# An encoder's MLP: its up projections with tokens on partitions, turned by VectorE and moved by GpSimd's DMA queue

## The chip, the cores and the metric

The kernel runs on one NeuronCore of a Trainium2 chip. The metric is the device time of one execution in microseconds (us); lower is better. A core has TensorE (PE, matrix products into PSUM), VectorE (DVE), ScalarE (ACT), GpSimd (POOL) and SyncE (SP); the last two also issue DMAs here, each on a queue of its own.

## The reference

Two layers on 256 tokens of 1024 channels, in float32. Each layer has a token mixer (pooling windows, dilated attention, gates) and then a gated MLP with a convolution of three tokens:

```python
def _conv_ffn(xn, w_up, conv_w, conv_b, w_down):
    a, gval = jnp.split(xn @ w_up, 2, axis=-1)          # D_FF = 2816 each
    a = depthwise_conv(a, conv_w, width 3, centred) + conv_b
    return (jax.nn.gelu(a) * gval) @ w_down

h = h + _token_mixer(_rmsnorm(h, norm1[layer]), ...)
h = h + _conv_ffn(_rmsnorm(h, norm2[layer]), ...)
```

The convolution runs over tokens, channel by channel.

## The kernel before

Channels are cut into blocks of 128: 8 for the model's width, 22 (NF) for D_FF. Every weight is read from HBM once, in loads of 1 MB. Each load is used as two pieces of 1024 values per partition. A piece is split into a high part (a rounding to the matrix engine's float32r, made by ScalarE, L179) and a low part (the rest, made by VectorE, L180). Activations are split in the same way, and a product is the sum of high x high, high x low and low x high. The class Weights keeps the order: `use` lists the pieces in the order of their use, `get` returns the next one and splits up to three ahead (LOOK = 3, five buffers BUFS, three load buffers RAW). A piece may go to a slot of an idle tile instead of one of the five buffers. A framework orders the instructions of each engine and sets the semaphores; tiles with one tag share a place in memory, so a new tile waits for the readers of the old one.

There are two forms of projection. `proj` (L489) has channels on the partitions of its result: the weight block stands in the array and the 256 tokens, high and low together 512 columns, stream through (L485); the weight's low part sees the high tokens alone, 256 columns (L487). `by_rows` (L587, through `v_sum` L577 and L582) has tokens on the partitions: a block of activations stands in the array and 512 columns of weights stream through, six matmuls for a piece and half of the tokens (t = 0, 1), four pieces for 512 columns. Its result must be turned before the convolution, which needs tokens in the free direction.

The MLP before the change takes the last four blocks of a (ENTRY = 4, the rest are FIRST = 18) by rows, at its start, in two PSUM tiles; ScalarE copies them, and VectorE turns them in 16 small transposes of 32 partitions (`blocks` L607, L612), one after each projection. All the other blocks, 18 of a and 22 of g, come from `proj`, two loads with 256 columns for two blocks. `up(f)` (L1124) adds the two sums of a block (ScalarE copies one, L507, VectorE adds the other, L508), convolves (L1134, L1135, L1138), applies the gelu by its tanh form (L1147 to L1152), multiplies by g (L1155), and splits the result (L1160, L1161). The down projection `residual_mm` (L516) takes one block per step: 12 matmuls of 512 columns (L512 to L514) into four PSUM tiles. It starts after block 6 (LAG) and goes on by two steps for every two blocks. The last four steps (`hold`) are held back, and are then run part by part, so that the norm of the first tokens can start early.

The mixer turns attention weights and its merged branch by VectorE's 32 x 32 transposes followed by `cross` (L599): 16 DMAs within SBUF that move each group of 32 partitions to its place, four after each visit, on SP's queue (L604). SP's queue also carries every load of weights (L119).

Of the kernel before, what the change touches and what calls it, by code (L numbers as in the profile page):

```python
# [10 lines left out]
F32 = mybir.dt.float32  # L11
# [24 lines left out]

WARM = (5, 1, 2, 1)
PAIRS = (2, 4, 0, 1, 3, 5)
LAG = 6
VISITS = ((0, 1, 12, 14), (2, 3, 15, 16), (9, 10, 22, 23), (10, 11, 23, 24))  # L40
ENTRY = 4
FIRST = NF - ENTRY
HALVES = (slice(0, 512), slice(512, D))
SEGMENTS = (HALVES, (slice(0, 512), slice(512, 768), slice(768, D)))

# [37 lines left out]
class Weights:  # L83
# [27 lines left out]
    def load(self, upto):  # L111
        while self.n_loaded < min(upto, len(self.loads)):
            src, shape, tag = self.loads[self.n_loaded]
            name = f"raw{self.n_loaded}"
            if tag is None:
                t = self.pool.tile([P, *shape], F32, tag="raw", bufs=self.RAW, name=name)
            else:
                t = self.idle.tile([P, *shape], F32, tag=tag, name=name)
            self.nc.sync.dma_start(out=t, in_=src)  # L119
            self.raw[self.n_loaded] = t  # L120
            self.n_loaded += 1

# [84 lines left out]
def encoder(ctx, tc, x, w_in, w_pool, pool_scale, w_a, w_b, w_o, norm1, norm2, w_up, conv_w,  # L207
# [28 lines left out]

    for l in range(DEPTH):
        for g in range(NG):
            c0 = C_V + g * 512
            slots = (("m2", 0, 2), ("m2", 1, 2), ("ybig",), ("at2",)) if g == 0 else ()  # L240
            for j in range(2):
                tag = "k1" if l == 0 and g == 1 and j == 0 else None
                W.use(rows(w_in[l], j * 512, 4, c0, 512, tag), slots[2 * j : 2 * j + 2])
        if l == 0:
            W.n_scaled = len(W.pieces)
        for c in range(3, -1, -1):
            W.use(cols(w_in[l], c * 256))
        for n, c in enumerate(PAIRS):
            q = cols(w_in[l], C_Q + c * 256)
            if n == 1:  # L250
                pool = W.add(
                    w_pool[l].rearrange("g (k p) c -> p (g k) c", p=P), (8, 256),
                    [((lambda t, j=j: t[:, 4 * j : 4 * j + 4, :]), (4, 256)) for j in range(2)],
                )
            k = cols(w_in[l], C_K + c * 256)
            if n == 1:
                k.insert(1, pool[0])
            if n == 2:
                q.insert(1, pool[1])
            W.use(q + k)  # L260
        def half_of(w, c0, half, n):
            for j in range(n):
                W.use(rows(w, j * 512, 4, c0 + half.start, 512))

        for half in HALVES:
            half_of(w_in[l], C_GP, half, 2)
        for half in HALVES:
            half_of(w_a[l], 0, half, 2)
            half_of(w_in[l], C_GA, half, 2)
            half_of(w_b[l], 0, half, 1)  # L270
        for c in range(4):
            W.use(rows(w_o[l], c * 256))
        slots = (("v1",), ("ybig",), ("at2",))
        for j in range(2):
            W.use(rows(w_up[l], j * 512, 4, FIRST * P, 512), slots[2 * j : 2 * j + 2])
        for f in range(0, NF, 2):
            a = cols(w_up[l], f * P) if f < FIRST else []
            g = cols(w_up[l], DFF + f * P)
            W.use([a[0], g[0], a[1], g[1]] if a else g)
            if f >= LAG:  # L280
                W.use(rows(w_down[l], (f - LAG) * P))
        for f in range(NF - LAG, NF, 2):
            W.use(rows(w_down[l], f * P))


    h = const.tile([P, 2, D], F32, name="h")
# [214 lines left out]
    def in_order(a):  # L501

        return a.rearrange("p (m t) -> p t m", t=2)

    def add_up(out, sums):

        nc.scalar.copy(out=out, in_=sums[1])  # L507
        nc.vector.tensor_add(out=out, in0=sums[0], in1=out)  # L508
# [65 lines left out]
    def v_tile():  # L574
        return acc.tile([P, 512], F32, tag="acc", name="v_ps")

    def v_sum(ps, x2, t, n, piece, of=4):  # L577

        _, (wh, wl) = piece
        passes = [(0, wh, 0), (0, wl, 0), (1, wh, 0), (0, wh, 1), (0, wl, 1), (1, wh, 1)]  # L580
        for m, (part, w, j) in enumerate(passes):
            nc.tensor.matmul(  # L582
                ps, x2[:, 2 * n + j, part, t, :], w[:, j, :], start=(n + m == 0),
                stop=(n == of - 1 and m == 5),
            )
# [13 lines left out]
    def cross(out, in_):  # L599

        for i in range(4):
            for j in range(4):
                a, b = slice(32 * i, 32 * i + 32), slice(32 * j, 32 * j + 32)
                nc.sync.dma_start(out=out[b, i], in_=in_[a, j])  # L604
            yield

    def blocks(out, in_):  # L607

        for i in range(4):
            for j in range(4):  # L610
                a, b = slice(32 * i, 32 * i + 32), slice(32 * j, 32 * j + 32)
                nc.vector.transpose(out=out[b, :, :, a], in_=in_[a, :, :, b])  # L612
                yield
# [166 lines left out]
    for l in range(DEPTH):  # L780
# [326 lines left out]
        acts = {}  # L1107


        a_last = big.tile([P, ENTRY, S], F32, tag="gates", name="a_last")  # L1110
        a_rows = big.tile([P, 2, ENTRY, P], F32, tag="m2", name="a_rows")

        held, ps = entry
        for t in range(2):
            if t:
                ps = v_tile()
                for n in range(4):
                    v_sum(ps, x2, t, n, held[n])
            nc.scalar.copy(out=a_rows[:, t], in_=ps)
        for i, _ in held:  # L1120
            W.free(i)
        turning = blocks(a_last.rearrange("p f (m t) -> p t f m", t=2), a_rows)

        def up(f):  # L1124
            w0, w1, w2, b = (prm[:, l, j * NF + f : j * NF + f + 1] for j in range(4))
            if f >= FIRST:
                a = a_last[:, f - FIRST, :]
            else:
                a = sm.tile([P, S], F32, tag="u", name="a")
                add_up(in_order(a), [halves(b) for b in proj(x2)])  # L1130
                next(turning, None)
            sums = proj(x2)
            y = sm.tile([P, S], F32, tag="s", name="y")
            nc.scalar.activation(y, a, AF.Identity, bias=b, scale=w1)  # L1134
# [3 lines left out]
            nc.vector.scalar_tensor_tensor(  # L1138
                out=y[:, : S - 1], in0=a[:, 1:], scalar=w2, in1=y[:, : S - 1],
                op0=ALU.mult, op1=ALU.add,  # L1140
            )
# [37 lines left out]
        for f in range(0, NF, 2):  # L1179
            up(f)  # L1180
            up(f + 1)
            if f >= LAG:
# [38 lines left out]
```

## Time and profile before

| | |
|---|---|
| median of 3 runs | 870.25 us (870.25 to 870.68) |
| the profiled execution | 870.25 us, of which its span is 868.5 us |
| granted TensorE clock | 0.998 |
| TensorE busy | 860.7 us |
| VectorE busy | 670.5 us |
| ScalarE busy | 496.8 us |
| GpSimd busy | 21.1 us |
| DMA | 167.23 MB, mean 193 GB/s |

The span runs from the first to the last instruction of the profiled execution. A group of the profile reads: line, engine, operation, result <- sources (partitions x elements) x count | busy us, mean ns of one | idle time of the engine just before, and what ended it. A row of a timeline reads: start, length, engine, line, operation. A matmul's end is modelled and overlaps the next one's start, so lengths add up to more than the time that passes. The chain of waits is followed back from the last instruction. A row of DMA issues ends with the size of one transfer and the median time from issue to landing.

### The profile page before, as it was taken

How to read it: one execution, taken by the hardware profiler on the slowest of the kernel's cores; microseconds unless marked ns; L12 is line 12 of the kernel's file. 1: busy time of each engine (PE TensorE's matmuls, PEld its weight loads, DVE VectorE, ACT ScalarE, POOL GpSimd, SP SyncE). 2: the span in 40 equal slices, each digit the busy share in tenths (PEclk: the TensorE clock that was granted, in tenths of full speed). 3: DMA queues.
4: the chain of work that ended last, by engine and by line, in shares of the span. 5: the costliest groups of instructions: out<-in, count | busy, mean ns of one | idle time of the engine just before them, and what ended most of it. 6: DMA issues, size and time to landing. Idle time of an engine off the chain costs nothing.

```text
span 868.5 us, 12204 instructions
## 1 busy us (share of the span) xinstructions
PE 860.7 (99%) x4554; PEld 740.9 (85%) x4554; DVE 670.5 (77%) x1084; ACT 496.8 (57%) x817; POOL 21.1 (2%) x53
## 2 busy tenths in 40 slices
PE   9999999999999999999999999999999999999997
PEld 7888988888888888888888899888888888888885
DVE  6998795756759997789756968775557799887884
ACT  6755644544646775667545555454445467666662
POOL 2020000000010000000000000000000000000000
PEclk9999999999999999999999999999999999999999
DMA  9676636664745565555626455547558255664631
GB/s 326 210 210 229 223 118 223 189 222 158 270 155 194 185 203 193 197 193 194 242 98 225 163 195 194 173 167 241 186 203 274 96 183 200 223 205 155 198 141 49
DMA packets 116095, 167.23 MB, mean 193 GB/s; under 512 B 4846, under 2 KB 81854, under 8 KB 116036
## 3 DMA queue, kind: packets, MB, share of 16 engines
q1 hardware_dynamic: 115524, 165.12, 56.6%
q0 software_dynamic: 496, 1.33, 0.6%
q8 instruction: 36, 0.59, 0.3%
q14 instruction: 23, 0.19, 0.1%
q10 hardware_dynamic: 16, 0.00, 0.0%
HBM read 160.12 MB, written 1.07 MB: 186 GB/s over the span
## 4 chain that ended last, share of the span: by engine, by line
PE 99%; ACT 0%; POOLq 0%; DVE 0%; issue 0%; POOL 0%; ACTq 0%
PE proj_ps L485 30%; PE rows_ps L582 18%; PE proj_ps L487 16%; PE res_ps L512 6%; PE res_ps L513 6%; PE v_ps L582 6%; PE res_ps L514 6%; PE v_ps L772 3%; PE v_ps L685 1%; PE o_ps L963 1%; PE s_ps L906 1%; PE o_ps L959 1%; PE s_ps L901 1%; PE xt_ps L453 1%; PE pool_ps L479 0%; PE pool_ps L478 0%
## 5 line engine op out<-in xcount | busy, mean ns | idle before, releaser
L180 DVE TENSOR_TENSOR wl<-raw,wh 128x1024 fp32r<-128x1024 f32 x274 | 333.1, 1222 | 121.0 <-ACT wh L179 118.4
L179 ACT CAST wh<-raw 128x1024 fp32r<-128x1024 f32 x274 | 285.6, 1049 | 173.0 <-PE proj_ps L485 64.7
L485 PE MATMUL proj_ps<-x,wh 128*128 128x512 f32 x1152 | 288.4, 392 | 0.0
L485 PEld LDWEIGHTS proj_ps<-x,wh 128*128 128x128 f32 x1152 | 208.2, 189 | 38.0
L487 PEld LDWEIGHTS proj_ps<-x,wl 128*128 128x128 f32 x1152 | 157.2, 190 | 11.3
L487 PE MATMUL proj_ps<-x,wl 128*128 128x256 f32 x1152 | 160.8, 282 | 0.0
L582 PE MATMUL rows_ps<-wh,x 128*128 128x512 f32 x256 | 82.1, 393 | 0.0
L512 PE MATMUL res_ps<-wh,actq 128*128 128x512 f32 (+1 forms) x184 | 70.2, 381 | 0.0
L513 PE MATMUL res_ps<-wl,actq 128*128 128x512 f32 (+1 forms) x184 | 70.1, 381 | 0.0
L514 PE MATMUL res_ps<-wh,actk 128*128 128x512 f32 (+1 forms) x184 | 69.9, 380 | 0.0
L582 PEld LDWEIGHTS rows_ps<-wh,x 128*128 128x128 f32 x256 | 47.9, 188 | 9.7
L582 PE MATMUL rows_ps<-wl,x 128*128 128x512 f32 x128 | 49.9, 389 | 0.0
L514 PEld LDWEIGHTS res_ps<-wh,actk 128*128 128x128 f32 x184 | 34.6, 188 | 6.7
L582 PE MATMUL rows_ps<-wh,po 128*128 128x512 f32 x128 | 40.1, 389 | 0.0
L512 PEld LDWEIGHTS res_ps<-wh,actq 128*128 128x128 f32 x184 | 34.7, 188 | 6.2
L513 PEld LDWEIGHTS res_ps<-wl,actq 128*128 128x128 f32 x184 | 34.7, 188 | 6.0
L1134 ACT ACTIVATE y<-a,prm 128x256 f32<-128x256 f32 x36 | 21.6, 600 | 21.9 <-DVE a L508 21.9
L1151 ACT ACTIVATE y<-y 128x256 f32<-128x256 f32 x44 | 18.3, 416 | 21.4 <-DVE y L1148 21.2
L582 PEld LDWEIGHTS rows_ps<-wh,po 128*128 128x128 f32 x128 | 24.0, 188 | 5.0
L582 PEld LDWEIGHTS rows_ps<-wl,x 128*128 128x128 f32 x128 | 24.1, 188 | 4.8
L512 PE MATMUL res_ps<-wh,m 128*128 128x512 f32 (+1 forms) x72 | 26.9, 374 | 0.0
L419 ACT ACTIVATE junk<-h 128x512 f32<-128x512 f32 (+1 forms) x20 | 10.9, 547 | 27.1 <-DVE h L417 27.1
(209 smaller groups left out, 1155.0 us busy)
## 6 DMA issues: line engine op xcount, KB each, us to landing
raw<-in_w_in_dram SPq DMA_DIRECT2D x58, 1024.0 KB, 5.2
raw<-in_w_up_dram SPq DMA_DIRECT2D x44, 1024.0 KB, 4.9
raw<-in_w_down_dram SPq DMA_DIRECT2D x22, 1024.0 KB, 4.9
raw<-in_w_a_dram SPq DMA_DIRECT2D x8, 1024.0 KB, 5.8
raw<-in_w_o_dram SPq DMA_DIRECT2D x8, 1024.0 KB, 7.1
pt<-rows SPq DMA_DIRECT2D x64, 64.0 KB, 3.7
raw<-in_w_b_dram SPq DMA_DIRECT2D x4, 1024.0 KB
raw<-in_w_pool_dram SPq DMA_DIRECT2D x2, 1024.0 KB
```

The source lines that it names most:

```text
L179: lambda: nc.scalar.copy(out=h, in_=src),
L180: lambda: nc.vector.tensor_sub(out=l, in0=src, in1=h.bitcast(F32)),
L419: nc.scalar.activation(junk[:, 0 : cc.stop - cc.start], h[:, t, cc], AF.Square, scale=D**-0.5, accum_out=ss[:, n : n + 1],)
L485: nc.tensor.matmul(ps, wh(k), x2[:, k], start=(k == 0), stop=False)
L487: nc.tensor.matmul(ps[:, 1], wl(k), x2[:, k, 0], start=False, stop=(k == nk - 1))
L512: nc.tensor.matmul(ps, ah, wh, start=first, stop=False)
L513: nc.tensor.matmul(ps, ah, wl, start=False, stop=False)
L514: nc.tensor.matmul(ps, al, wh, start=False, stop=last)
L582: nc.tensor.matmul(ps, x2[:, 2 * n + j, part, t, :], w[:, j, :], start=(n + m == 0), stop=(n == of - 1 and m == 5),)
L772: nc.tensor.matmul(ps[t], a[:, k, t, :], w[:, j, :], start=(k + m == 0), stop=(k == KD - 1 and m == 2),)
L1134: nc.scalar.activation(y, a, AF.Identity, bias=b, scale=w1)
L1151: nc.scalar.activation(y2, y2, AF.Tanh, scale=c)
```

## The change

All of the up projection goes by rows, in eleven sets of 512 columns per layer: a0 to a4 and g0 to g4 with four blocks each, and r5 with the last two blocks of a and of g (its two loads of 1 MB are cut in two halves each). ORDER gives the order of sets and of groups of four down steps (d0 to d4). A unit is one weight piece. CHUNKS gives for each block the unit after which `up` is called. At a set's end VectorE turns both PSUM tiles (one for each half of the tokens) in 32 x 32 blocks into one of two buffers (`up_at2`), and `cross` moves the blocks: for a and r into a tile in the place of `gates` or `v0`, for g into one of two buffers in the place of `xn`. `up` then starts with a scalar copy that brings a into token order (in place of the two sums), and multiplies by g straight from the turned tile; the factor 0.5 of the gelu moves from that product into the split. `cross` issues on GpSimd's queue in place of SP's, in the mixer too.

```diff
-LAG = 6
+ORDER = "a0 g0 a1 g1 a2 g2 d0 a3 g3 d1 a4 g4 r5 d2 d3 d4"
+CHUNKS = (13, 15, 17, 19, 21, 23, 25, 27, 29, 31, 33, 35, 41, 43, 45, 47, 53, 54, 56, 57, 58, 60)
-ENTRY = 4
-FIRST = NF - ENTRY
...
     def cross(out, in_):
         for i in range(4):
             for j in range(4):
                 a, b = slice(32 * i, 32 * i + 32), slice(32 * j, 32 * j + 32)
-                nc.sync.dma_start(out=out[b, i], in_=in_[a, j])
+                nc.gpsimd.dma_start(out=out[b, i], in_=in_[a, j])
             yield
...
+        def turn_up(key, ps, tag):
+            if not ways:
+                for own in ("at2", "xn"):
+                    t = big.tile([P, 2, 4, 2, 4, 32], F32, tag=own, name="up_" + own)
+                    ways.append([t[:, 0], t[:, 1]])
+            rows = ways[0].pop(0)
+            ways[0].append(rows)
+            if tag is None:
+                out = ways[1].pop(0)
+                ways[1].append(out)
+            else:
+                out = big.tile([P, 4, 2, 4, 32], F32, tag=tag, name="up_turned")
+            for t in range(2):
+                nc.vector.transpose(
+                    out=rows[:, :, t].rearrange("p j c r -> p c j r"),
+                    in_=ps[t].rearrange("p (c j r) -> p c j r", c=4, j=4),
+                )
+            run(cross(out, rows))
+            turned[key] = out.rearrange("p i t c r -> p c t i r")
...
         def up(f):
-            if f >= FIRST:
-                a = a_last[:, f - FIRST, :]
-            else:
-                a = sm.tile([P, S], F32, tag="u", name="a")
-                add_up(in_order(a), [halves(b) for b in proj(x2)])
-                next(turning, None)
-            sums = proj(x2)
+            n, c = divmod(f, 4)
+            av, gv = (turned["r", n][:, j + c] if n == 5 else turned[k, n][:, c] for k, j in (("a", 0), ("g", 2)))
+            a = sm.tile([P, S], F32, tag="u", name="a")
+            nc.scalar.copy(out=blocks_in_order(a), in_=av)
...
-            g = sm.tile([P, 2, P], F32, tag="p", bufs=3, name="g")
-            add_up(g, [halves(a) for a in sums])
...
-            nc.vector.scalar_tensor_tensor(
-                out=g, in0=in_order(y2), scalar=0.5, in1=g, op0=ALU.mult, op1=ALU.mult
-            )
+            g = sm.tile([P, 2, P], F32, tag="p", bufs=3, name="g")
+            nc.vector.tensor_mul(out=g.rearrange("p t (i r) -> p t i r", i=4), in0=blocks_in_order(y2), in1=gv)
...
-            nc.scalar.copy(out=ah, in_=g)
-            nc.vector.tensor_sub(out=al, in0=g, in1=ah.bitcast(F32))
+            nc.scalar.mul(out=ah, in_=g, mul=0.5)
+            nc.vector.scalar_tensor_tensor(
+                out=al, in0=g, scalar=0.5, in1=ah.bitcast(F32), op0=ALU.mult, op1=ALU.subtract
+            )
...
-        for f in range(0, NF, 2):
-            up(f)
-            up(f + 1)
-            if f >= LAG:
-                next(down)
-                next(down)
+        def unit():
+            nonlocal count, chunk
+            count += 1
+            while chunk < NF and CHUNKS[chunk] < count:
+                up(chunk)
+                chunk += 1
+
+        for kind, n in ORDER.split():
+            if kind == "d":
+                for _ in range(4):
+                    next(down)
+                    unit()
+                continue
+            if (kind, n) == ("a", "0"):
+                held, ps = entry
+                ps = [ps, v_tile()]
+                for k in range(4):
+                    v_sum(ps[1], x2, 1, k, held[k])
+                    unit()
+                for i, _ in held:
+                    W.free(i)
+            else:
+                ps = by_rows(x2, 4, unit)
+            n = int(n)
+            turn_up((kind, n), ps, None if kind == "g" else ("gates", "v0")[n % 2])
```

The list of weight pieces follows ORDER, with rows of 512 columns for a and g. In the changed kernel `cross` stands at L611 (its DMA at L616), `turn_up` at L1124, the scalar copy of a at L1154, the product with g at L1176, and the matmuls by rows at L594.

More of the change, by code (lines that the diff above doesn't have):

```diff
@@ L118, in load @@
                 t = self.idle.tile([P, *shape], F32, tag=tag, name=name)
-            self.nc.sync.dma_start(out=t, in_=src)
+            parts = [(t[:, :, j], one) for j, one in enumerate(src)] if type(src) is tuple else [(t, src)]
+            for out, one in parts:
+                self.nc.sync.dma_start(out=out, in_=one)
             self.raw[self.n_loaded] = t
@@ L273, in encoder @@
         slots = (("v1",), ("ybig",), ("at2",))
-        for j in range(2):
-            W.use(rows(w_up[l], j * 512, 4, FIRST * P, 512), slots[2 * j : 2 * j + 2])
-        for f in range(0, NF, 2):
-            a = cols(w_up[l], f * P) if f < FIRST else []
-            g = cols(w_up[l], DFF + f * P)
-            W.use([a[0], g[0], a[1], g[1]] if a else g)
-            if f >= LAG:
-                W.use(rows(w_down[l], (f - LAG) * P))
-        for f in range(NF - LAG, NF, 2):
-            W.use(rows(w_down[l], f * P))
+        for kind, n in ORDER.split():
+            n = int(n)
+            for j in range(2):
+                if kind == "d":
+                    W.use(rows(w_down[l], (4 * n + 2 * j) * P))
+                elif kind == "r":
+                    src = w_up[l][j * 512 : (j + 1) * 512].rearrange("(k p) c -> p k c", p=P)
+                    c0 = (4 * n * P, 4 * n * P + DFF)
+                    W.use(
+                        W.add(
+                            tuple(src[:, :, c : c + 256] for c in c0), (4, 2, 256),
+                            [
+                                ((lambda t, j=j: t[:, 2 * j : 2 * j + 2].rearrange("p k h c -> p k (h c)")), (2, 512))
+                                for j in (0, 1)
+                            ],
+                        )
+                    )
+                else:
+                    p = rows(w_up[l], j * 512, 4, (kind == "g") * DFF + 4 * n * P, 512)
+                    W.use(p, slots[2 * j : 2 * j + 2] if (kind, n) == ("a", 0) else ())
+        W.use(rows(w_down[l], (NF - 2) * P))
     h = const.tile([P, 2, D], F32, name="h")
@@ L1107, in encoder, with blocks_in_order @@
         acts = {}
[L1110 to L1122, printed above, removed]
+        turned, ways = {}, []
+        def turn_up(key, ps, tag):
[14 more added lines that the diff above has]
+                    in_=ps[t].rearrange("p (c j r) -> p c j r", c=4, j=4),
+                )
+            run(cross(out, rows))
+            turned[key] = out.rearrange("p i t c r -> p c t i r")
+        def blocks_in_order(a):
+            return a.rearrange("p (i r t) -> p t i r", i=4, t=2)
         def up(f):
             w0, w1, w2, b = (prm[:, l, j * NF + f : j * NF + f + 1] for j in range(4))
-            if f >= FIRST:
-                a = a_last[:, f - FIRST, :]
-            else:
-                a = sm.tile([P, S], F32, tag="u", name="a")
-                add_up(in_order(a), [halves(b) for b in proj(x2)])
-                next(turning, None)
-            sums = proj(x2)
+            n, c = divmod(f, 4)
+            av, gv = (turned["r", n][:, j + c] if n == 5 else turned[k, n][:, c] for k, j in (("a", 0), ("g", 2)))
+            a = sm.tile([P, S], F32, tag="u", name="a")
+            nc.scalar.copy(out=blocks_in_order(a), in_=av)
             y = sm.tile([P, S], F32, tag="s", name="y")
@@ L1154, in up @@
             )
-            nc.vector.scalar_tensor_tensor(
-                out=g, in0=in_order(y2), scalar=0.5, in1=g, op0=ALU.mult, op1=ALU.mult
-            )
+            g = sm.tile([P, 2, P], F32, tag="p", bufs=3, name="g")
+            nc.vector.tensor_mul(out=g.rearrange("p t (i r) -> p t i r", i=4), in0=blocks_in_order(y2), in1=gv)
             n = f % NH
             ah, al = (x[n >= HPG][:, n - HPG * (n >= HPG)] for x in (acth, actl))
-            nc.scalar.copy(out=ah, in_=g)
-            nc.vector.tensor_sub(out=al, in0=g, in1=ah.bitcast(F32))
+            nc.scalar.mul(out=ah, in_=g, mul=0.5)
+            nc.vector.scalar_tensor_tensor(
+                out=al, in0=g, scalar=0.5, in1=ah.bitcast(F32), op0=ALU.mult, op1=ALU.subtract
+            )
             acts[f] = (ah, al)
@@ L1178, in encoder @@
         )
-        for f in range(0, NF, 2):
-            up(f)
-            up(f + 1)
-            if f >= LAG:
-                next(down)
-                next(down)
+        count, chunk = 0, 0
+        def unit():
[4 more added lines that the diff above has]
+                chunk += 1
+        for kind, n in ORDER.split():
+            if kind == "d":
+                for _ in range(4):
[10 more added lines that the diff above has]
+                    W.free(i)
+            else:
+                ps = by_rows(x2, 4, unit)
+            n = int(n)
+            turn_up((kind, n), ps, None if kind == "g" else ("gates", "v0")[n % 2])
+        assert chunk == NF
         if l + 1 < DEPTH:
```

## The prediction, made before the result was known

> **What bounds the kernel now.** I read the page's busy shares and chain of waits first, then the costliest groups by line with shapes kept apart, then timelines for the distance from one instruction's start to the next one's, last the DMA issues.
>
> ```profile
> span 868.5 us, 12204 instructions
> PE 860.7 (99%) x4554; PEld 740.9 (85%) x4554; DVE 670.5 (77%) x1084; ACT 496.8 (57%) x817; POOL 21.1 (2%) x53
> PE   9999999999999999999999999999999999999997
> PE 99%; ACT 0%; POOLq 0%; DVE 0%; issue 0%; POOL 0%; ACTq 0%
> PE proj_ps L485 30%; PE rows_ps L582 18%; PE proj_ps L487 16%; PE res_ps L512 6%; PE res_ps L513 6%; PE v_ps L582 6%; PE res_ps L514 6%; PE v_ps L772 3%; PE v_ps L685 1%; PE o_ps L963 1%; PE s_ps L906 1%; PE o_ps L959 1%; PE s_ps L901 1%; PE xt_ps L453 1%; PE pool_ps L479 0%; PE pool_ps L478 0%
> ```
>
> TensorE is busy in every slice and is 99% of the chain: no stall is left to remove, so the change can win only by asking TensorE for less, and can lose wherever its new steps come late. The shares are overlapping busy times, so the price of a piece of work must come from start to start:
>
> ```profile
> 299.95 2.00 PE L485 MATMUL proj_ps<-x,wh 128*128 128x512 f32 x8
> 302.74 2.00 PE L485 MATMUL proj_ps<-x,wh 128*128 128x512 f32 x8
> 308.33 0.40 PE L512 MATMUL res_ps<-wh,actq 128*128 128x512 f32 x1
> 313.79 1.98 PE L485 MATMUL proj_ps<-x,wh 128*128 128x512 f32 x8
> 187.29 40.85 PE rows_ps L582 x180
> 227.98 0.39 PE L512 MATMUL res_ps<-wh,m 128*128 128x512 f32 x1
> ```
>
> One projection (8 matmuls of 512 columns, 8 of 256, one weight piece) takes 302.74 - 299.95 = 2.79 us. Two down pieces (24 matmuls of 512) take 313.79 - 308.33 = 5.46, so 2.73 each. The form that the change brings in exists already in the mixer: 180 matmuls from 187.29 to 227.98, 0.226 each, 2.71 for a piece's 12. I call one weight piece a unit.
>
> **TensorE's part.** In each layer 40 projections (18 for a, 22 for g) become 40 units by rows; four were by rows before. 40 x (2.79 - 2.71) = 3.2 us a layer, **6.4 us** in all. This is on the path: TensorE sets the end.
>
> **Vector and scalar part.** Gone per channel block: the two adds of L508 with their scalar copies L507. Gone per layer: 16 small transposes. New: two transposes from PSUM per set of 512 columns, 22 a layer; the last product and the subtraction keep their shapes.
>
> ```profile
> L508 DVE TENSOR_TENSOR g<-proj_ps,g 128x256 f32<-128x256 f32 x44 | 18.4, 418 | 0.0
> L612 DVE STREAM_TRANSPOSE a_last<-a_rows 32x256 f32<-32x256 f32 x32 | 14.0, 436 | 0.7
> L935 DVE STREAM_TRANSPOSE rows<-probs 128x1024 f32<-128x1024 f32 x8 | 9.9, 1237 | 0.1
> 300.12 1.22 DVE L180 TENSOR_TENSOR wl<-raw,wh 128x1024 fp32r<-128x1024 f32 x1
> 301.26 0.48 DVE L1138 SCALAR_TENSOR_TENSOR y<-a,prm,y 128x255 f32<-128x255 f32 x1
> 301.65 0.41 DVE L508 TENSOR_TENSOR g<-proj_ps,g 128x256 f32<-128x256 f32 x1
> 307.58 0.41 DVE L508 TENSOR_TENSOR g<-proj_ps,g 128x256 f32<-128x256 f32 x1
> 307.91 1.21 DVE L180 TENSOR_TENSOR wl<-raw,wh 128x1024 fp32r<-128x1024 f32 x1
> ```
>
> Start to start, a split holds VectorE 1.14 us, a convolution step 0.39, a 256-column step 0.33. A transpose of 512 columns lies between 436 ns for 256 and 1237 for 1024: 0.70 on the line, 0.62 start to start. None reads PSUM, so the ends are 0.44 and 1.24; I take 0.70, as VectorE's adds cost the same from either memory (L508 reads PSUM at 418 ns for 256). One block now needs 2 x 0.39 + 4 x 0.33 = 2.10. Where sets and blocks overlap (one block every two units by CHUNKS) two units ask VectorE for 2 x 1.14 + 2.10 + 0.62 = 5.00 us of 5.42: covered, but only 0.42 us is left to catch up with. Beside down pieces it is 4.38 of 5.46. ScalarE goes from six to five steps per block and isn't near its limit. This part costs nothing while VectorE never waits long.
>
> **The new wait.** Each set crosses by 16 DMAs of 32 KB on GpSimd's queue: 11 x 16 = 176 a layer, and the mixer's 48 a layer move there from SP's. In the built program each issue also waits for the landing of the one eight before it. No row shows this form on that queue; the nearest:
>
> ```profile
> L392 POOL DMA_DIRECT2D fd<-fsb x3: 523/542/746, 52.5 to 54.1; - x3
> L395 POOL DMA_DIRECT2D bt<-fd x5: 749/749/807, 56.1 to 59.1; - x5
> fd<-fsb POOLq DMA_DIRECT2D x2, 4.0 KB, 2.4
> fd<-fsb POOLq DMA_DIRECT2D x1, 12.0 KB, 3.3
> bt<-fd POOLq DMA_DIRECT2D x5, 256.0 KB, 7.1
> way<-way SPq DMA_DIRECT2D x32, 32.0 KB, 2.5
> 205.34 7.49 SPq L604 DMA_DIRECT2D way<-way  x12
> ```
>
> An issue costs 0.523 us for 4 runs of 1 KB and up to 0.807 for 512 runs of 512 bytes; 32 runs of 1 KB lie near the first, and by the count of runs at 0.54. I take **0.55**, and keep 0.523 and 0.807 as ends. Landing: the same transfer took 2.5 us on SP, small ones 2.0 to 3.3 on GpSimd's queue; I take 2.5 from its issue, 2.0 after it (eight issues take 4.4, so the wait for the one eight before is idle). A set then crosses in 16 x 0.55 + 2.0 = 10.8 us, and the queue is held 8.8 of the 10.85 that TensorE needs for a set.
>
> Who waits: ScalarE's first copy of a block (for a) and VectorE's product (for g); behind them in order stand the casts and splits of the weights, three pieces ahead of TensorE (8 us). At the start, g0's sums end at unit 8, land about 13 us later (2 for transposes, 10.8), and the next piece behind the product is the first of a2, needed 8 units = 21.7 us after: hidden. The narrow place is the **layer's end**. r5 ends at unit 52; then 10 whole down pieces (27.3) and 3 parts of 0.68 pass before the last split is needed: 29.3 us. Against it: transposes with their queue 2.3, crossing 10.8, then blocks 20 and 21, five splits and two for the next layer, 7 x 1.14 + 2 x 2.10 = 12.2, with some 2 us of waits between scalar and vector steps. 27.3 of 29.3: it fits with 2 us. So at 0.55 the wait costs nothing.
>
> SP's part: 44 loads for w_up remain, in rows of 2 KB in place of 1 KB (the r loads are cut in two halves), and the 96 crossings that stood between loads leave that queue. TensorE's chain holds no wait for a load now, so I count nothing. The mixer's crossings, 0.62 us each on SP (7.49 for 12), are issued four to a visit and read two visits later; at 0.55 they keep that cover, at 0.807 they'd lose 0.7 us a visit, still inside 5 us.
>
> **Sum.** Profiled execution 870.25 us, span 868.5, 1.75 around it; the median is also 870.25. 870.25 - 6.4 = 863.85: I forecast **864 us**.
>
> **A rule that speaks against the change.** If a VectorE instruction could hold up the issues, each would wait for its end, as long as a split: 1.22 us. In the trace:
>
> ```profile
> 52.46 1.29 POOL L392 DMA_DIRECT2D fd<-fsb  x2 [9.42 <-DVE fsb L386]
> 56.06 3.79 POOL L395 DMA_DIRECT2D bt<-fd  x5 [1.45 <-DMA fd<-fsb]
> 56.02 1.22 DVE L180 TENSOR_TENSOR wl<-raw,wh 128x1024 fp32r<-128x1024 f32 x1
> 57.76 1.22 DVE L180 TENSOR_TENSOR wl<-raw,wh 128x1024 fp32r<-128x1024 f32 x1
> ```
>
> Five issues ran in 3.79 us beside splits without any one stretching to 1.22. The Trainium skill (SBUF — State Buffer, Who interferes with whom) says that GpSimd's DMAs need descriptors written by GpSimd, that a VectorE copy or tensor-scalar step in a two-port mode locks it out, and advises issuing from SP or ScalarE instead; by the same section a two-input step takes only the read side. By that the trace agrees, since the steps above and in the MLP have two inputs or read PSUM.
>
> **Rivals.** Lateness has one law here. Per two sets (eight units) issues at T cost 32 x (T - 0.55) more than planned and VectorE regains 4 x 0.42 = 1.7; the down groups d0 and d1 regain 2.2 each; five pairs a layer. Up to T = 0.60 nothing builds up.
>
> - *Slightly slow issues*, T about 0.62 to 0.68. At 0.65: 5 x (3.2 - 1.7) - 4.4 = 3.1 a layer, 863.85 + 6 = 870; at 0.68, 880. For it: GpSimd's first issue took 746 ns with only 4 runs. Against: the next two took 542 and 523. 0.21.
> - *Issues at bt's price* (ends on the other side): T = 0.749: 5 x (6.4 - 1.7) - 4.4 = 19 a layer, **902 us**; at 0.807, 920. VectorE and ScalarE stand at a set that hasn't landed, the splits queue up behind, TensorE starves. It decides from T = 0.60. For it: five of eight issues took this. Against: they had 16 times as many runs. 0.10.
> - *Lockout*: T = 1.22: 5 x (21.4 - 1.7) - 4.4 = 94 a layer, 1052 us. 0.03, as the rows above speak against it.
> - *VectorE becomes the bound*: transposes at 1.24 instead of 0.70 give 5.54 of 5.42 per two units; with chain waits some 1 to 4 us a layer, about 868. 0.06.
> - *The change doesn't do what it says*: rows cost 2.79 here as projections did; 870. 0.02, since 180 matmuls show 2.71.
>
> **How the numbers follow.** Forecast 863 to 867: 0.58. This kernel's measurement tells about 0.2% (1.7 us) from no change. Faster is the forecast, 0.58. Same takes 0.08 of the slightly slow issues, 0.03 of VectorE's case and 0.02 of the last: 0.13. Slower takes 0.13, 0.03, 0.10 and 0.03: 0.29. The range, 862.5 to 882, leaves out bt's price, the lockout and the far end of slightly slow issues, about 0.18. The forecast's own range is 863 to 867.
>
> **What would show it.** TensorE: L594's units at 2.71 us in the MLP, proj_ps gone there; its slices still at 9. GpSimd: issue at 0.52 to 0.60 us and landing near 2.5. VectorE: transposes near 0.70 us and no long idle ahead of L1176; ScalarE none ahead of L1154. The forecast is wrong if issues exceed 0.60 us, landings 3.5 us, or if TensorE has gaps ahead of the last down pieces, which would say that the 2 us at the layer's end were not there.

## The result, and the profile after

The changed kernel takes 896.91 us (median of 4 runs, 895.3 to 897.82), against 870.25 us before: ratio 1.0303, 95% interval 1.0286 to 1.0321. The forecast was 864.0 us. The profiled execution is 897.2 us with a span of 895.4. First the page of the profile after: its head, two rows of the slices, and the chain of waits.

```profile
span 895.4 us, 11904 instructions
...
PE 867.4 (97%) x4234; PEld 727.5 (81%) x4234; DVE 651.7 (73%) x1016; ACT 483.7 (54%) x777; POOL 239.8 (27%) x501
...
PE   9999999999999999999799999999999999989994
...
PEclk9999999999999999999799999999999999999998
...
PE 4%; DMA 3%; DVE 3%; ACT 1%; POOL 1%; issue 1%; POOLq 0%; DVEq 0%; ACTq 0%
```

TensorE has 320 matmuls fewer and yet 6.7 us more of busy time, and its slices now have holes: the clock row falls in the same slice (425 to 448 us) as the busy row. The chain of waits, which before the change was TensorE for 99%, can now be followed back through 13% of the span only, and passes through transfers, VectorE, ScalarE and GpSimd. The groups by line say who stands for whom:

```profile
L594 PE MATMUL rows_ps<-wl,x 128*128 128x512 f32 x448 | 175.6, 392 | 5.6 <-DVE wl L181 5.5
L616 POOL DMA_DIRECT2D up_turned<-up_at x192 | 94.0, 498 | 140.9 <-issue 75.4
...
L1154 ACT COPY a<-up_turned 128x256 f32<-128x256 f32 x44 | 17.5, 415 | 73.1 <-DMA up_turned<-up_at 36.8
```

An issue on GpSimd's queue takes 0.498 us, less than the 0.55 taken. ScalarE stands 73.1 us in front of the copy that reads a crossed set, and TensorE waits for splits made behind that copy. Now one set, a4 of the first layer, through its engines. VectorE turns it:

```profile
382.57 1.30 DVE L1138 STREAM_TRANSPOSE up_at<-rows_ps 128x512 f32<-128x512 f32 x2
...
398.40 1.22 DVE L181 TENSOR_TENSOR wl<-raw,wh 128x1024 fp32r<-128x1024 f32 x1 [8.79 <-ACT wh L180]
```

GpSimd issues its 16 crossings, then those of g4 (in brackets the idle time ahead of a row, and who ended it):

```profile
384.41 5.86 POOL L616 DMA_DIRECT2D up_turned<-up_at  x12 [15.84 <-issue]
392.12 0.50 POOL L616 DMA_DIRECT2D up_turned<-up_at  x1 [1.86 <-DMA up_turned<-up_at]
393.04 1.47 POOL L616 DMA_DIRECT2D up_turned<-up_at  x3 [0.42 <-DMA up_turned<-up_at]
394.92 7.82 POOL L616 DMA_DIRECT2D up_xn<-up_at  x16 [0.40 <-issue]
```

SP issues three loads of weights in the same stretch (380 to 400 us):

```profile
382.67 6.11 SPq L120 DMA_DIRECT2D raw<-in_w_down_dram  x3
```

ScalarE gets to its copy of the set:

```profile
397.01 0.42 ACT L1154 COPY a<-up_turned 128x256 f32<-128x256 f32 x1 [11.37 <-DMA up_xn<-up_at]
```

The answer on DMA for the stretch with these loads, 384 to 394.8 us: the queues' packets, MB and shares of the 16 engines (q1 is SP's, q0 GpSimd's), and the median from issue to landing:

```profile
q1 hardware_dynamic: 795, 3.08, 82.2%
q0 software_dynamic: 421, 0.44, 12.7%
...
up_turned<-up_at POOLq DMA_DIRECT2D x16, 32.0 KB, 4.8
```

The same for the stretch behind them, 394.8 to 402.3 us:

```profile
q0 software_dynamic: 507, 0.51, 24.3%
q1 hardware_dynamic: 7, 0.01, 0.5%
...
up_xn<-up_at POOLq DMA_DIRECT2D x16, 32.0 KB, 1.7
```

The same transfer lands 1.7 us after its issue when SP's queue is empty and 4.8 us after it when loads run. In this set the landings come in three bursts, at 388, 392 to 393 and 394 to 397 us, which fits one behind each load. The thirteenth issue has to wait for the fifth to land (1.86 us). The set has crossed 397.0 - 383.9 = 13.1 us after its transposes, where 10.8 had been planned; ScalarE has then stood for 11.4 us, VectorE for 8.8, and TensorE's next matmuls come 1.5 us late. (The view names a transfer of g4's at the end of ScalarE's wait; the copy reads up_turned, whose last crossing of this set lands at 396.9.) Read in this way for all 22 sets, a crossing takes 10.9 to 16.6 us, median 13.3. The page has the same for the whole execution: SP's share, the loads, and the crossings of a (up_turned) and g (up_xn).

```profile
q1 hardware_dynamic: 92548, 159.87, 53.1%
...
raw<-in_w_up_dram SPq DMA_DIRECT2D x40, 1024.0 KB, 5.7
...
up_turned<-up_at POOLq DMA_DIRECT2D x192, 32.0 KB, 4.1
up_xn<-up_at POOLq DMA_DIRECT2D x160, 32.0 KB, 1.7
```

Where the time went by stage (first matmul of each MLP to the next stage's, then from the last matmul to the end; from the timeline of each profiled execution):

| kernel | MLP 1 | MLP 2 | last matmul to end | time, us | ratio |
|---|---|---|---|---|---|
| before | 184.5 | 183.9 | 6.5 | 870.25 | |
| after | 198.7 | 191.9 | 10.5 | 896.9 | 1.030 |
| e1, no crossings in the MLP | 181.6 | 180.9 | 11.4 | 870.0 | 1.000 (0.999 to 1.001) |
| e2, crossings on SP | 206.9 | 206.0 | 6.1 | 913.9 | 1.051 (1.049 to 1.054) |
| e3, before with GpSimd's queue | 184.5 | 183.8 | 11.4 | 876.6 | 1.008 (1.006 to 1.009) |
| e4, two queues | 181.7 | 180.9 | 12.0 | 870.5 | 1.001 (1.000 to 1.002) |
| e5, two queues, last norm elsewhere | 181.7 | 180.9 | 5.8 | **864.2** | **0.994** (0.992 to 0.995) |
| e6, half of the loads' bytes | 181.6 | 180.9 | 10.5 | 872.0 | 1.003 (1.002 to 1.004) |
| e7, loads in quarters | 195.8 | 187.8 | 10.5 | 893.8 | 1.028 (1.026 to 1.029) |
| e8, d1 behind r5 | 191.0 | 189.5 | 10.5 | 886.8 | 1.019 (1.018 to 1.021) |
| e9, held queue | 219.8 | 214.6 | 5.9 | 936.7 | 1.078 (1.075 to 1.082) |
| e10, 32 crossings of before on GpSimd | 185.0 | 183.9 | 6.5 | 870.6 (one run) | |
| e11, 16 of them | 184.5 | 183.9 | 6.5 | 869.7 (one run) | |
| e12, held less | 207.5 | 200.3 | 5.9 | 911.7 | 1.049 (1.047 to 1.050) |

The span grew by 26.9 us: 14.2 in the first MLP, 8.1 in the second, 4.0 behind the last matmul, 0.6 in the first mixer.

### The profile page after: what moved, and what is told of

It reads as the page before. It is cut to its first block, busy times and chain, and to the rows that moved or that the text cites. A ratio compares the mean times of both kernels' runs of the same rounds, so it can differ in the third digit from the quotient of the medians.

```text
span 895.4 us, 11904 instructions
## 1 busy us (share of the span) xinstructions
PE 867.4 (97%) x4234; PEld 727.5 (81%) x4234; DVE 651.7 (73%) x1016; ACT 483.7 (54%) x777; POOL 239.8 (27%) x501
## 5 line engine op out<-in xcount | busy, mean ns | idle before, releaser
L594 PE MATMUL rows_ps<-wh,x 128*128 128x512 f32 x896 | 281.3, 392 | 0.6 <-ACT wh L180 0.6
L594 PEld LDWEIGHTS rows_ps<-wh,x 128*128 128x128 f32 x896 | 169.1, 189 | 36.0 <-ACT wh L180 1.1
L594 PE MATMUL rows_ps<-wl,x 128*128 128x512 f32 x448 | 175.6, 392 | 5.6 <-DVE wl L181 5.5
L616 POOL DMA_DIRECT2D up_turned<-up_at x192 | 94.0, 498 | 140.9 <-issue 75.4
L497 PE MATMUL proj_ps<-x,wh 128*128 128x512 f32 x512 | 128.8, 393 | 0.0
L497 PEld LDWEIGHTS proj_ps<-x,wh 128*128 128x128 f32 x512 | 92.0, 189 | 16.5
L594 PEld LDWEIGHTS rows_ps<-wl,x 128*128 128x128 f32 x448 | 84.5, 189 | 25.0 <-DVE wl L181 7.6
L616 POOL DMA_DIRECT2D pt<-rows x64 | 31.5, 499 | 246.4 <-ACT q L1021 110.9
L616 POOL DMA_DIRECT2D up_xn<-up_at x160 | 78.2, 497 | 18.0 <-DVE up_at L1138 4.4
L499 PEld LDWEIGHTS proj_ps<-x,wl 128*128 128x128 f32 x512 | 69.9, 190 | 5.1
L499 PE MATMUL proj_ps<-x,wl 128*128 128x256 f32 x512 | 71.5, 282 | 0.0
L1154 ACT COPY a<-up_turned 128x256 f32<-128x256 f32 x44 | 17.5, 415 | 73.1 <-DMA up_turned<-up_at 36.8
L525 PEld LDWEIGHTS res_ps<-wl,actq 128*128 128x128 f32 x184 | 35.6, 194 | 17.7 <-DVE wl L181 10.8
L594 PE MATMUL rows_ps<-wh,po 128*128 128x512 f32 x128 | 40.1, 389 | 0.0
```

Source lines behind the costliest of these rows:

```text
L497: nc.tensor.matmul(ps, wh(k), x2[:, k], start=(k == 0), stop=False)
L499: nc.tensor.matmul(ps[:, 1], wl(k), x2[:, k, 0], start=False, stop=(k == nk - 1))
L525: nc.tensor.matmul(ps, ah, wl, start=False, stop=False)
L594: nc.tensor.matmul(ps, x2[:, 2 * n + j, part, t, :], w[:, j, :], start=(n + m == 0), stop=(n == of - 1 and m == 5),)
L616: nc.gpsimd.dma_start(out=out[b, i], in_=in_[a, j])
L1154: nc.scalar.copy(out=blocks_in_order(a), in_=av)
```

## The experiments

Three theories. A: the crossings land late, since loads hold the DMA engines, and with eight in flight each round of eight waits again. B: GpSimd's own time for a set is too long. C: the new order is late by itself, on VectorE or ScalarE.

**e1, the MLP's crossings left out.**

```diff
-                    out=rows[:, :, t].rearrange("p j c r -> p c j r"),
+                    out=out[:, :, t].rearrange("p j c r -> p c j r"),
...
-            run(cross(out, rows))
```

> Leaves out the crossings of the MLP: VectorE's transposes write straight to the tile that `up` reads, so the blocks of 32 partitions stay where they are and the output isn't the reference's; all other work, the mixer's crossings on GpSimd's queue included, stays. Theory A (the crossings land late, because a 1 MB load holds the DMA engines and only eight crossings are in flight): no stall is left, each MLP takes 181.3 us from its first matmul to the next layer's (184.5 before, less 3.2), GpSimd's closing drain falls from 8.3 us towards the 1.4 of before as 96 of 448 DMAs are left on that queue; 864 to 867 us. Theory C (the new order of blocks, the transposes or the splits behind them are late by themselves, on VectorE or ScalarE): the gaps stay, 885 to 897 us.

Measured 870.0 us. Both MLPs have the length of the working to 0.3 us (184.5 - 3.2 = 181.3, 183.9 - 3.2 = 180.7), the clock is back and no hole is left, as its page shows:

```profile
PE   9999999999999999999999999999999999999994
...
PEclk9999999999999999999999999999999999999997
```

Theory C falls: transposes, blocks and splits fit. The time missed the expectation by 3 us, because the drain didn't shrink with the number of DMAs: the end still took 11.4 us.

**e2, all crossings on SP's queue**, one word of L616 (`nc.sync`).

> All crossings issued on SP's queue, as before the change; the rest as changed. Theory B (GpSimd's queue itself is what is late: its issues, its descriptors): without it the stalls go, and its drain too, 864 to 868 us. Theory A: the transfers stay 16 for a set, at most eight in flight and now in one count with the loads of weights, and stand in one queue with them, so landings don't get earlier and loads get later: 885 to 930 us, less the 4 us of GpSimd's drain.

913.9 us, as A had it: worse, without any crossing on GpSimd's queue. A row of SP's timeline in e2:

```profile
303.29 13.61 SPq L616 DMA_DIRECT2D up_xn<-up_at  x16
```

Its DMA issues, the loads of w_up:

```profile
raw<-in_w_up_dram SPq DMA_DIRECT2D x40, 1024.0 KB, 7.1
```

One set holds SP's queue for 13.6 us, in which no load can be issued, and the loads land 7.1 us after their issue (5.7 after the change, 4.9 before).

**e3, the kernel before with its 96 mixer crossings on GpSimd's queue**, the same word in the other direction.

> The kernel before with one part of the change alone: the mixer's 96 crossings on GpSimd's queue. The mixer's stretches were 0.6 us longer after the change, in the first layer alone, and GpSimd's closing drain took 8.3 us in place of 1.4. If the drain goes with the number of DMAs on that queue (96 of 448): 870.25 + 0.6 + 1.5, about 872 us. If it is there whenever the queue was used at this length: 875 to 877. Both theories on the MLP say the same here.

876.6 us: the mixers hardly change (the second is 0.9 us longer), but the end does. GpSimd's closing instruction in e3, in the view of its line (the last of the three figures is the longest, in ns; the two times behind are the first and the last start):

```profile
L1216 POOLq DRAIN  x3: 40/102/9194, 864.6 to 874.3; - x3
```

The same in the kernel before:

```profile
L1216 POOLq DRAIN  x3: 40/102/1358, 863.4 to 868.2; - x3
```

And after the change:

```profile
L1259 POOLq DRAIN  x3: 40/102/8294, 886.3 to 895.2; - x3
```

Of the 26.9 us after the change 4.0 are this drain: it begins with GpSimd's last instruction, the last norm's root, and takes 8.3 us in place of 1.4.

**e4, every second crossing on SP's queue.**

```diff
-                nc.gpsimd.dma_start(out=out[b, i], in_=in_[a, j])
+                (nc.sync, nc.gpsimd)[j % 2].dma_start(out=out[b, i], in_=in_[a, j])
```

> Every second crossing on SP's queue, the others on GpSimd's, so that up to 16 can be in flight (eight of each kind), a whole set. Theory A: a set is late by one load at most, 5 to 6 us, in place of two in turn, about 10 us for a set; most of the stalls go: 866 to 882 us. Theory B: GpSimd issues half as many, 864 to 870 us. Theory C: no change but for the drain, 888 to 897 us.

870.5 us: the stalls are gone from both MLPs; what is left over the forecast is the drain (12.0 us of end). The single landing is hardly faster: the crossings of a have a median of 4.1 us on SP's queue (as far as the profile tells their landings) and 3.7 on GpSimd's. But all 16 of a set are issued 5 to 8.5 us after its transposes, against 8.1 to 13.5 after the change.

**e5, the same, with the last norm's sums and root off GpSimd.**

```diff
-                nc.gpsimd.tensor_tensor(out=r, in0=ss[:, 3:4], in1=mhalf, op=ALU.pow)
+                if self.last:
+                    nc.scalar.activation(r, ss[:, 3:4], AF.Sqrt)
+                    nc.vector.reciprocal(r, r)
+                else:
+                    nc.gpsimd.tensor_tensor(out=r, in0=ss[:, 3:4], in1=mhalf, op=ALU.pow)
```

> As e4, and the sums and the root of the last norm alone move from GpSimd to VectorE (its two sums) and ScalarE with VectorE (a square root, then a reciprocal), so that GpSimd's last instruction is its last crossing, some 40 us ahead of the end. In e4 GpSimd's closing drain took 9.8 us and began only after that norm's root; from TensorE's last matmul to the end passed 12.0 us, against 6.5 before. If the drain runs as soon as GpSimd has nothing left to issue, it is hidden: 870.5 - 5.5 = 865.0, between 864.3 and 866. If it runs only at the program's end, whatever came before: 870 to 871.

864.23 us (863.98 to 864.77), just under the expected stretch and faster than both kernels: 5.4 us less than the runs of before beside it (869.61). The row of TensorE on its page:

```profile
PE   9999999999999999999999999999999999999997
```

Its drain:

```profile
L1264 POOLq DRAIN  x3: 40/102/10039, 822.6 to 861.9; - x3
```

ScalarE's only waits for crossed sets (us in total, times, longest):

```profile
ACT a L1159 <- DMA up_turned<-up_at: 5.4, 6, 2.2
```

The drain is as long as ever, 10.0 us, but starts near 823 and is over long before the end.

**e6, half of the bytes of the loads of w_up and w_down.**

```diff
+                    half = shape[0] // 2
+                    out, one = out[:, :half], one[:, :half]
```

> The changed kernel with half of the bytes of each whole load of w_up and w_down left out (both pieces of a load are cut from its first half, so the output isn't the reference's; the two halves of r5's loads stay whole). Nothing of GpSimd's queue changes. Theory A: a load holds the DMA engines for half as long, so a crossing that comes upon one lands about 2.5 us sooner: median landing of up_turned 2 to 3 us in place of 4.1, each MLP 181.5 to 185 us, in all 869 to 878 us (the drain of 5 us stays). If the landings were late for another reason (GpSimd's descriptors, VectorE beside them): median 4, each MLP as after, 890 to 898 us.

872.0 us, and both MLPs at 181.6 and 180.9. GpSimd still issues 16 crossings per set at 0.5 us each; only the loads are shorter. The DMA issues of e6:

```profile
up_turned<-up_at POOLq DMA_DIRECT2D x192, 32.0 KB, 2.4
up_xn<-up_at POOLq DMA_DIRECT2D x160, 32.0 KB, 1.8
```

ScalarE's waits in e6:

```profile
ACT a L1159 <- DMA up_turned<-up_at: 16.8, 6, 6.6
ACT a L1159 <- DMA up_xn<-up_at: 8.9, 2, 5.8
```

So theory B's time of issue isn't enough for a stall, and the loads are what makes the landings late. A set now crosses in 9.3 to 13.7 us, median 9.9; ScalarE stands up to 6.6 us and TensorE never: that much the splits made ahead cover.

**e7, each 1 MB load as four of 256 KB.**

```diff
+                    for k in range(shape[0]):
+                        for c in range(0, shape[1], 512):
+                            self.nc.sync.dma_start(out=out[:, k, c : c + 512], in_=one[:, k, c : c + 512])
```

> The changed kernel with each load of w_up and w_down of 1 MB issued as four of 256 KB on the same queue; the bytes are the same. If a DMA engine serves one transfer to its end and then turns to the other queue, a crossing waits for 1.2 us at most in place of 4 to 5: median landing 2 to 3 us, the stalls go but for little, 869 to 880 us. If crossings wait until SP's queue holds nothing, whatever the size of its transfers: landings as after, 890 to 900 us.

893.8 us; the stalls stay, and so do the landings of e7:

```profile
raw<-in_w_up_dram SPq DMA_DIRECT2D x160, 256.0 KB, 4.3
...
up_turned<-up_at POOLq DMA_DIRECT2D x192, 32.0 KB, 4.2
```

The time is the one expected for crossings that wait until SP's queue is empty, but the packets say otherwise. In e7 both queues move packets side by side, here from 353 to 358 us:

```profile
q1 hardware_dynamic: 833, 1.53, 87.7%
q0 software_dynamic: 153, 0.15, 8.8%
```

After the change there are such stretches too, but also stretches in which GpSimd's queue moves nothing beside a load, as from 384.6 to 386.4 us, where the answer has this row alone although crossings of a4 are issued from 384.4 on and one alone lands 1.7 us later:

```profile
q1 hardware_dynamic: 180, 0.74, 101.3%
```

So shorter loads let crossings pass beside them, but slowly: 0.15 MB in 5 us is less than five crossings, where GpSimd can issue ten. The median stays where it was. In e6, which halves the bytes, it falls.

**e8, d1 behind r5.**

```diff
-ORDER = "a0 g0 a1 g1 a2 g2 d0 a3 g3 d1 a4 g4 r5 d2 d3 d4"
+ORDER = "a0 g0 a1 g1 a2 g2 d0 a3 g3 a4 g4 r5 d1 d2 d3 d4"
```

> The changed kernel with the group d1 of four down steps moved behind r5 (a0 g0 a1 g1 a2 g2 d0 a3 g3 a4 g4 r5 d1 d2 d3 d4), and blocks 16 to 21 begun after units 50, 51, 53, 54, 55 and 57: four units, 10.9 us, more between the last set and the step that needs its last blocks; crossings and queue are as after. Theory A (the delay of a set is bounded, at most two loads, about 5 us more than planned): the gaps ahead of the last down steps go (6 and 3 us, with the low clock behind them about 10 and 4), those of the middle stay: 878 to 888 us. If the crossings fall behind further with every set (the queue is too slow on the whole), the gaps stay whatever the room: 890 to 900 us.

886.8 us, inside A's range: the first MLP's gaps from d2 on shrank from 7.7 us to 0.8; 2.9 us came up in d1, and those in the middle stayed. Lateness doesn't grow from set to set, so the queue is not too slow on the whole; it is each set that is late.

**e9 and e12, two queues with a dummy step of GpSimd for each of its crossings**, a power in e9, an addition in e12, both on e5.

```diff
+                if j % 2:
+                    nc.gpsimd.tensor_tensor(out=idle, in0=in_[:, j].rearrange(way_of(in_))[:, 0:1], in1=mhalf, op=ALU.pow)
```

> As e5, with a dummy step of GpSimd for each of its crossings (a power of one column, 0.57 us), so that GpSimd's queue is held about as long for a set as after the change (8 x 0.5 + 8 x 0.57 = 8.6 us against 16 x 0.5 = 7.9), while no more than eight of its crossings, one set's share, are in flight. Theory A (it was the wait for the landing of the crossing eight places before, each round of eight up to 6 us): the time stays near that of e5, 864 to 868 us. Theory B (it was GpSimd's own time per set): the stalls come back, 880 to 897 us.

> As e9 with a shorter dummy step (an addition of one column): in e9 the eight dummies ran ahead of the eight issues and took 6.4 to 8.5 us, so a set held GpSimd for 10.4 to 12.5 us, about the 10.85 that TensorE takes for one and more, which the theories don't differ on. Here a dummy should take 0.2 to 0.45 us, and a set hold GpSimd for 5.5 to 7.6 us, at most what 16 issues of 0.496 us take (7.9), with the eight real issues last. Theory A (the waits for landings among the issues, not the time of the issues): 864 to 868 us. Theory B (GpSimd's own time per set): 875 to 897 us.

936.7 and 911.7 us: the ranges of both theories missed both runs, and in e12 theory A is plainly wrong as it stands in the expectation. The dummies ran ahead of the issues. GpSimd's timeline in e12 for set a4:

```profile
390.38 5.27 POOL L629 TENSOR_TENSOR idle<-up_at,mhalf 128x1 f32<-128x1 f32 x7 [21.28 <-DVE up_at L1151]
395.59 3.94 POOL L627 DMA_DIRECT2D up_turned<-up_at  x8
```

ScalarE's copy of that set:

```profile
405.35 0.73 ACT L1167 COPY a<-up_turned 128x256 f32<-128x256 f32 x2 [11.02 <-DMA raw<-in_w_down_dram]
```

The dummies took up to 0.75 us each (5.27 for seven) where 0.20 to 0.45 had been expected. Four crossings land within 2.4 us, the other four meet the next load and take 5.1 to 5.9; ScalarE gets the set 14.5 us after its transposes (405.35 - 390.84), and the stalls are back, without any wait among the issues. So the waits for the eighth before aren't needed for a stall. In every kernel a crossing is a sum: queue time, plus waits among the issues, plus the last landing. Where its median over the sets is about 10 us (e6) or less (e4, e5), TensorE doesn't stall; at 13 us (after, e7, e8) it does. The crossing alone doesn't tell how much is lost: e12's median is 11.9 us, as far as its trace tells the landings, and its MLPs are longer than after's. VectorE stands 60.5 us there in front of a block's first step of the convolution, against 22.0 after the change, so more than the crossing differs. e9 and e12 are no clean test of theory B either, since they hold GpSimd up to 9.2 us and more for a set in one piece ahead of the last issue.

**e10 and e11, the kernel before with 32 and 16 crossings on GpSimd's queue.**

> The kernel before, with the crossings of the mixer's merged branch alone (16 a layer, 32 in all) on GpSimd's queue. The closing drain took 1.36 us with 8 DMAs on that queue, 9.19 with 104, 9.77 with 232 and 8.29 with 456. If it grows with the DMAs up to a limit: about 3 to 4 us with 40, and 871.5 to 873 us in all. If it is long once the queue has been used so: 9 us, 875 to 877.

> The same in the first layer only: 16 crossings, 24 DMAs in all on GpSimd's queue. If the drain grows with the DMAs: about 2.5 us, 871 to 872 us in all; if not: 9 us, 875 to 877.

The drain of e10:

```profile
L1216 POOLq DRAIN  x3: 40/102/3966, 863.8 to 868.5; - x3
```

And of e11:

```profile
L1216 POOLq DRAIN  x3: 40/102/2659, 862.9 to 867.7; - x3
```

With 8, 24, 40 and 104 DMAs on that queue the drain takes 1.36, 2.66, 3.97 and 9.19 us: 0.082 us for each. Beyond that it levels off (8.3 to 10.7 in the kernels with 232 and 456). The times were below the expectation, at 870.6 and 869.7: a drain up to 4 us lies beside the landing of the output, whose end stays 6.5 us behind the last matmul.

## Why the prediction was wrong, step by step

- **TensorE's part: right.** A unit by rows cost 2.72 us (240 matmuls from 264.21 to 318.61), 2.71 had been taken. e1, e4, e5 and e6 show both MLPs shorter by 2.8 to 3.0 us, 3.2 had been taken, and e5, without the stalls and with the drain hidden, comes within 0.3 us of the forecast's 864.0.
- **VectorE's part: right.** The transposes after the change, in the view of their line (min/median/max, ns), where 0.70 us had been taken:

```profile
L1138 DVE STREAM_TRANSPOSE up_at<-rows_ps x40: 666/704/718, 274.8 to 852.0; 128x512 f32<-128x512 f32 x40
```

  In e1 VectorE does all the new work and TensorE never waits.
- **T, the issue: right on the safe side**, 0.496 us against 0.55. The case at bt's price (T = 0.749) and the lockout didn't happen, though the former's time, 902 us, is close to the result. It was the same place, late sets with the splits queued up behind them, for another cause. The rule on VectorE locking out descriptor writing (the Trainium skill, SBUF — State Buffer, Who interferes with whom) had no effect to be seen, as the prediction expected: the issues took 496 ns in the median and 588 at most, beside whatever VectorE did. Its way out, issuing from SP, made this kernel slower (e2).
- **"I take 2.5 from its issue, 2.0 after it (eight issues take 4.4, so the wait for the one eight before is idle)": this step failed.** The landing was measured at 4.1 us for the sets of a (1.7 to 6.7) and 1.7 for those of g. The 2.5 came from way<-way before the change, on SP's own queue; the step didn't ask what a transfer of another queue does beside 1 MB loads that take up 53% of the engines' time. With 4 to 6 us, the wait isn't idle either, and a set crosses in 13.3 us in place of 10.8. GpSimd's waits for its own landings (us in total, times, longest):

```profile
POOL up_turned L616 <- DMA up_turned<-up_at: 16.9, 14, 2.6
```

  e6 shows the cause by itself: half of the loads' bytes, same queue, same issues, no stall. The prediction had named landings over 3.5 us as what would make it wrong, but had no rival for them.
- **"27.3 of 29.3: it fits with 2 us": wrong by what follows from the step above.** Its working set r5 alone against d2 to d4. But a4's lateness had by then made ScalarE and VectorE stand, so that r5's transposes began 8.2 us after its last matmul (398.1); ScalarE got it 25 us after that, and TensorE had gaps of 7.7 us in the last down steps (start to start, less 0.23 for each matmul). VectorE's row:

```profile
406.32 0.72 DVE L1138 STREAM_TRANSPOSE up_at<-rows_ps 128x512 f32<-128x512 f32 x1
```

  ScalarE's copy of r5:

```profile
423.41 0.73 ACT L1154 COPY a<-up_turned 128x256 f32<-128x256 f32 x2 [5.67 <-DMA up_turned<-up_at]
```

  Nor was the layer's end the only narrow place. The working showed cover for a crossing at the start alone and left out those between. In the second layer the largest hole, 4.6 us from one matmul to the next, lies in the middle, at 781 us: the set g2 crosses in 16.6 us, and VectorE stands in front of its product with the splits behind it:

```profile
783.39 0.76 DVE L1176 TENSOR_TENSOR g<-y,up_xn 128x256 f32<-128x256 f32 x2 [5.57 <-DMA up_xn<-up_at]
```
- **SP's queue and the mixer at nothing: right** within 0.6 us. The loads land later (5.7 us against 4.9), but ScalarE's casts wait 2.1 us in all for loads of w_up and w_down, against 2.7 before.
- **Two terms were not in the sum at all**: the slow clock behind gaps (6.8 us at most, worked out in the last section) and the drain (4 us).

The sum as it was: 863.85 by the working; + 17.4 and 11.2 in the two MLPs (198.7 - 181.3 and 191.9 - 180.7); + 4.0 of drain; + 0.6 in the first mixer: 897.05, and the profiled execution took 897.2.

What stays open: how much of e4's gain comes from the shorter queue and how much from the waits that went; why set a2's ninth issue came 3.2 us after the landing that it needed; and why the first MLP loses 6 us more than the second (the half clock would explain 3.4 of them).

## What to carry to other kernels

The time of a transfer is to be taken from a row with the same queue and the same company: a 32 KB move took 1.7 us alone and up to 6.7 beside loads on another queue. Where many small transfers make up one result, count how many can be in flight and add up queue time, waits and the last landing; spreading them over two queues was worth 26 us here (896.9 to 870.5). A gap on TensorE can cost more than its length, since the clock may fall behind it (here up to 6.8 of the 28.6 us lost in the MLPs). An engine's closing work is to be started early.

## What the hardware showed that was not expected

- **The clock falls in a row of short gaps.** After, in stretches cut where the clock changes (columns: length, PE busy, PEld, DVE, ACT, POOL, then the granted clock, DMA share and GB/s):

```profile
424.20:427.40 3.20, 0.88 (x3) 0.19 (x1) 2.73 (x5) 2.67 (x5) 0.00 (x0) 1.00 0.00 0
427.40:430.80 3.40, 3.18 (x8) 2.51 (x9) 3.26 (x12) 2.87 (x5) 0.00 (x0) 0.50 0.61 185
...
437.60:444.40 6.80, 5.91 (x14) 4.64 (x15) 4.77 (x5) 3.66 (x5) 0.28 (x1) 0.50 0.89 319
785.80:789.20 3.40, 3.40 (x8) 2.71 (x9) 3.40 (x9) 2.04 (x5) 0.00 (x0) 0.50 0.00 1
```

  From 424.2 on the starts of four matmuls lie 1.9, 1.5 and 0.6 us apart, and the clock is at half for 3.4 us; from 433.2 to 438.5 they lie up to 1.7 us apart, and it is at half for 6.8 us; behind the hole of 4.6 us in the second MLP for 3.4. Elsewhere in the MLPs it is at 1.00. So 13.6 us at half clock cost 6.8 us at most of the 28.6 lost there; the rest is waiting. TensorE's busy time misleads here: it is 13.1 us above that of e1 for the same 4234 matmuls, but the modelled end of a matmul ahead of a gap counts as busy too.
- **GpSimd's transfers get little beside SP's loads.** The rows shown with e7 have both ends: after the change nothing for 1.8 us beside a load of 1 MB, in e7 8.8% of the engines' time beside loads in quarters. The Trainium skill (DMA: Bandwidth & Descriptors, Queues, rings and completion order) says that an engine goes round the queues that have work and takes a whole packet, typically 9 to 17 descriptors, from one before it turns to the next. The turns in e7 agree with it in kind. How much of a load makes one such packet, and so how long a crossing has to wait for its turn, no run here shows.
- **A queue of GpSimd that has been used costs at the end**: 0.082 us for each DMA, up to some 10 us, beginning with GpSimd's last instruction.
